# Seven products for eight in two column groups of each SwiGLU, in a float32 decoder trunk on one Trainium2 core

## The chip, the core and the metric

The kernel runs on one core of one Trainium2 chip. The core has a matrix engine (PE, with PEld for its weight loads), a vector engine (DVE), an activation engine (ACT), a general engine (POOL) and a sequencer (SP) that issues most transfers; sixteen DMA engines move the data. Each engine works through its own queue in order. The metric is the device time of one execution in microseconds (us), as a median of runs.

## What is computed

Two layers (DEPTH) over 256 tokens of width 1024. A layer is a half-step SwiGLU, a mixer of three branches, and a second half-step SwiGLU:

```python
def swiglu_ffn(h, w_in, w_out):
    gate, up = jnp.split(h @ w_in, 2, axis=-1)
    return (jax.nn.silu(gate) * up) @ w_out

for l in range(DEPTH):
    x = x + FFN_RESID * swiglu_ffn(rms_norm(x, ffn1_norm[l]), ffn1_w_in[l], ffn1_w_out[l])
...
    x = x + FFN_RESID * swiglu_ffn(rms_norm(x, ffn2_norm[l]), ffn2_w_in[l], ffn2_w_out[l])
```

w_in is 1024 x 5632 (2816 gate columns, then 2816 up columns), w_out 2816 x 1024, all in float32. So there are four SwiGLUs: a first and a second in each layer.

## The kernel before

**Precision.** Every large product is made of three matmuls in a rounded float32 (mm3x, L128): both operands are cut into a rounded high part and the rest, and high x high, high x low and low x high are added in PSUM. The weights are cut on the chip: split (L100) casts a chunk on ACT (whi, L106) and subtracts on DVE (wlo, L107).

**Stream.** All weights lie in one array, in the order of use, in chunks of at most 128 x 1024 (512 KB). load (L87) has SP fetch them into five raw buffers; prefetch cuts up to three chunks ahead of the one in use, into four whi and four wlo buffers. next_sub gives PE its next chunk.

**A SwiGLU** (ffn, L274). The first product runs over 11 groups of 512 columns, 256 of gate and the matching 256 of up. A group is four chunks; a chunk holds two row blocks of 128, and for each of them and each half of the tokens three matmuls of 512 columns are issued, twelve in all. Two PSUM banks (ps_in) collect the two token halves; acc has four banks, so that a group is read out while the next is computed. ACT makes SILU of the gate half (L302), DVE multiplies by up (L304); the result is turned by PE (ps_a, L269) and cut again (L270, L271) for the second product (ps_out), which adds to x.

**Norm.** rms_norm's gain goes into the cut of x (Norm.split: xg, L235 on ACT, L236 on DVE). The row factor rc = rs_x comes from sums of squares (xsq, L250) by POOL (L210) and is applied when a group is read out. The second half of x's columns is turned and cut only when the first chunk of the next stage has been issued (late).

**Order.** A scheduler lays out each engine's queue from the program's order and its own estimates; the splits have a higher priority. A tile's buffer is given by its tag, and a later tile with the same tag waits until the earlier one is done with: xbc, vg, zt, big12a and big12b are buffers that the mixer uses and a SwiGLU does not.

## Time and profile before

| | |
|---|---|
| median of 3 runs | 1265.35 us (1263.08 to 1266.62) |
| the profiled execution, its time | 1265.64 us |
| the profiled execution, its span | 1263.9 us |
| DVE, ACT busy | 63%, 53% of the span |
| weights and the rest read from HBM | 219.46 MB |

The page counts busy time by engine and cuts the span into 40 slices; DMA there is the mean busy share of the sixteen DMA engines:

```profile
DMA  8665564634554445555555555545455544555662
```

A row of a group reads: line, engine, operation, out<-in, shape, count, then busy us and mean ns of one, then the idle time of the engine just before, with what ended it. A row of the timeline reads: start, duration, engine, line, operation.

### The profile page before, as it was taken

To read this page: it belongs to the slowest core of one execution; us is meant where nothing else is said; L and a number is where in the kernel's file an instruction comes from. 1 tells how busy PE (TensorE), PEld (TensorE's weight loads), DVE (VectorE), ACT (ScalarE), POOL (GpSimd) and SP (SyncE) were. 2 spreads that over 40 slices of the span, in tenths; PEclk is the share of its full clock that TensorE was granted. 3 is DMA by queue.
4 is the path that set the end of the run, shared out by engine and by line. 5 is a ranking of instruction groups with operands and counts; after the bars stand their busy time and mean duration, and the time that the engine had idled before them with its cause. 6 is when DMAs were issued, how large, how long until landed. Compare 5 with 4: busy or idle time off the path is not lost.

```text
span 1263.9 us, 16712 instructions
## 1 busy us (share of the span) xinstructions
PE 1237.6 (98%) x6332; PEld 1042.4 (82%) x6332; DVE 791.8 (63%) x1099; ACT 667.9 (53%) x908; POOL 120.6 (10%) x108
## 2 busy tenths in 40 slices
PE   9999999999999999999999999999999999999998
PEld 6888889988887778888888888898988877888886
DVE  6555557888756665555556555588795576555553
ACT  7545445647666454444455444456567744545532
POOL 0000004423200000000000000064150000000000
PEclk9999999989999999999999999999999999999999
DMA  8665564634554445555555555545455544555662
GB/s 326 212 185 183 193 188 125 212 100 159 195 173 151 149 167 185 186 186 192 184 183 184 184 186 193 187 124 184 123 165 184 150 153 163 171 185 187 183 191 83
DMA packets 62432, 221.59 MB, mean 175 GB/s; under 512 B 7056, under 2 KB 7184, under 8 KB 62224
## 3 DMA queue, kind: packets, MB, share of 16 engines
q1 hardware_dynamic: 61488, 219.40, 52.9%
q10 hardware_dynamic: 864, 1.13, 0.3%
q8 instruction: 49, 0.80, 0.3%
q14 instruction: 31, 0.25, 0.1%
HBM read 219.46 MB, written 1.05 MB: 174 GB/s over the span
## 4 chain that ended last, share of the span: by engine, by line
PE 90%; DVE 4%; POOL 2%; issue 2%; ACT 1%; DMA 1%; SPq 0%; DVEq 0%; ACTq 0%; POOLq 0%
PE ps_in L131 12%; PE ps_in L130 12%; PE ps_in L132 12%; PE ps_out L132 7%; PE ps_out L130 7%; PE ps_out L131 7%; PE ps_g L131 3%; PE ps_g L130 3%; PE ps_g L132 3%; PE ps_in L126 2%; PE ps_in L124 2%; PE ps_in L125 2%; DVE wlo L107 2%; PE ps_a L269 2%; PE ps_br L130 1%
## 5 line engine op out<-in xcount | busy, mean ns | idle before, releaser
L107 DVE TENSOR_TENSOR wlo<-raw,whi 128x1024 fp32r<-128x1024 f32 (+3 forms) x417 | 513.6, 1235 | 364.8 <-ACT whi L106 363.7
L106 ACT CAST whi<-raw 128x1024 fp32r<-128x1024 f32 (+3 forms) x417 | 431.3, 1039 | 388.3 <-PE ps_in L132 156.4
L131 PE MATMUL ps_in<-wlo,xg 128*128 128x512 f32 x704 | 278.8, 396 | 0.9 <-DVE wlo L107 0.9
L130 PE MATMUL ps_in<-whi,xg 128*128 128x512 f32 x704 | 276.1, 396 | 2.2 <-ACT xg L235 1.2
L132 PE MATMUL ps_in<-whi,xg 128*128 128x512 f32 x704 | 273.6, 391 | 0.0
L130 PEld LDWEIGHTS ps_in<-whi,xg 128*128 128x128 f32 x704 | 131.9, 188 | 33.4 <-ACT whi L106 1.8
L131 PEld LDWEIGHTS ps_in<-wlo,xg 128*128 128x128 f32 x704 | 132.3, 188 | 27.2 <-DVE wlo L107 2.5
L132 PEld LDWEIGHTS ps_in<-whi,xg 128*128 128x128 f32 x704 | 132.0, 188 | 26.4
L126 PE MATMUL ps_in<-xg,wlo 128*128 128x256 f32 x336 | 96.4, 288 | 1.5 <-DVE wlo L107 1.5
L124 PE MATMUL ps_in<-xg,whi 128*128 128x256 f32 x336 | 95.1, 289 | 1.1 <-ACT whi L106 0.9
L125 PE MATMUL ps_in<-xg,whi 128*128 128x256 f32 x336 | 96.2, 288 | 0.0
L131 PE MATMUL ps_out<-wlo,aa 128*128 128x512 f32 x192 | 75.8, 395 | 0.0
L131 PE MATMUL ps_g<-wlo,xg 128*128 128x512 f32 x192 | 75.8, 395 | 0.0
L130 PE MATMUL ps_out<-whi,aa 128*128 128x512 f32 x192 | 75.5, 393 | 0.0
L132 PE MATMUL ps_g<-whi,xg 128*128 128x512 f32 x192 | 75.1, 391 | 0.0
L132 PE MATMUL ps_out<-whi,aa 128*128 128x512 f32 x192 | 74.8, 389 | 0.0
L210 POOL TENSOR_TENSOR rs_x<-ms_x,mhalf 128x2 f32<-128x2 f32 x6 | 4.2, 698 | 724.4 <-DVE ms_x L208 722.8
L130 PE MATMUL ps_g<-whi,xg 128*128 128x512 f32 x192 | 72.7, 394 | 0.0
L126 PEld LDWEIGHTS ps_in<-xg,wlo 128*128 128x128 f32 x336 | 65.3, 194 | 1.9 <-DVE wlo L107 1.9
L124 PEld LDWEIGHTS ps_in<-xg,whi 128*128 128x128 f32 x336 | 64.4, 194 | 2.0 <-ACT whi L106 1.9
L125 PEld LDWEIGHTS ps_in<-xg,whi 128*128 128x128 f32 x336 | 65.4, 195 | 0.7 <-issue 0.3
L130 PE MATMUL ps_out<-whi,ab 128*128 128x512 f32 x160 | 62.2, 389 | 0.0
(269 smaller groups left out, 1791.8 us busy)
## 6 DMA issues: line engine op xcount, KB each, us to landing
raw<-in_w SPq DMA_DIRECT2D x397, 512.0 KB, 3.5
raw<-in_w SPq DMA_DIRECT2D x8, 414.0 KB, 3.3
raw<-in_w SPq DMA_DIRECT2D x6, 384.0 KB, 3.0
raw<-in_w SPq DMA_DIRECT2D x4, 276.0 KB, 3.0
x<-in_xT SPq DMA_DIRECT2D x4, 256.0 KB, 4.7
x<-in_x SPq DMA_DIRECT2D x1, 1024.0 KB, 8.8
out_x<-x ACTq DMA_DIRECT2D x4, 256.0 KB, 3.7
row<-in_prow SPq DMA_DIRECT2D x2, 360.0 KB, 6.6
```

The lines of the kernel that those rows point to most:

```text
L106: act.copy(hi[:, a:b], r[:, a:b])
L107: dve.tensor_tensor(lo[:, a:b], r[:, a:b], hi[:, a:b].bitcast(F32), ALU.subtract)
L124: pe.matmul(ps, lhsT=whi, rhs=xhl[:, 0], start=first, stop=False)
L125: pe.matmul(ps, lhsT=whi, rhs=xhl[:, 1], start=False, stop=False)
L126: pe.matmul(ps, lhsT=wlo, rhs=xhl[:, 0], start=False, stop=last)
L130: pe.matmul(ps, lhsT=xhi, rhs=whi, start=first, stop=False)
L131: pe.matmul(ps, lhsT=xhi, rhs=wlo, start=False, stop=False)
L132: pe.matmul(ps, lhsT=xlo, rhs=whi, start=False, stop=last)
L210: pool.tensor_tensor(r, m, mhalf[:, :n], ALU.pow)
L269: pe.transpose(ps[:, i, halves(b)], parts[b][:, P * i : P * (i + 1)], ident)
```

## The change

The first product of each SwiGLU keeps seven of its eleven groups ("narrow", 28 chunks). The other four become two groups of 1024 columns ("wide", 512 of gate and 512 of up), computed by Strassen's form in Winograd's version. The tokens and the rows are halved, so that the input is x11, x12, x21, x22 (the first index is the token half; 128 tokens x 512 features each), and the weights of a wide group are b11, b12 (rows 0 to 511: gate, up) and b21, b22 (rows 512 to 1023). Instead of eight products of a block of x with a block of b there are seven, with b11, t1 = b11 + b12, t2 = b11 + b12 + b22, t3 = b12 + b22, b22, b21 and t4 = t2 + b21, the up columns carried with a minus sign that is taken back at the end (nrc). Each product is two chunks of six matmuls.

- **Weight sums.** t1 and t3 (tiles xsum, ysum) are made by transfers: SP loads b11 or b22 a second time, and POOL issues a transfer that adds b12 to it. t2 and t4 are made by DVE additions in place (L196, L189). All seven are cut like other chunks: a SwiGLU's first product has 56 splits, where it had 44. The raw buffers of b11 are held until t2 is made. SP fetches 40 raw chunks for it, where it had 44, and eight 512 KB loads for the sums; eight adding transfers follow on POOL.
- **Input sums.** Norm keeps a full copy of the scaled x (xgf, one more ACT activation for each block of 128 columns); combined forms four sums of its blocks on DVE and cuts them (xs).
- **Results.** Two banks of acc (ps_wa, ps_wd) are held by a wide group and accumulate several products; ACT copies ps_wa out in between (m, u, v), DVE adds ps_wd and ps_we. Two banks are left for a narrow group.
- **Order.** The wide products stand between narrow chunks: two narrow chunks behind each of the seven in the first wide group, and 2, 1, 1, 2, 1, 1, 2 in the second.
- aside and the turns of the results move to other places in the loop; the stream is packed in the new order.

The core of the diff:

```diff
+NARROW = 7
+WIDE = 2
+def _ffn_order():
+    narrow = [("n", g, c) for g in range(NARROW) for c in range(4)]
+    gaps = [[2] * 7, [2, 1, 1, 2, 1, 1, 2]]
+    order, narrow = narrow[:4], narrow[4:]
+    for j in range(WIDE):
+        for names, n in zip((("b11", "b12"), ("t1",), ("t2",), ("t3",), ("b22",), ("b21",), ("t4",)), gaps[j]):
+            order += [(name, j, c) for name in names for c in range(2)]
+            order += narrow[:n]
+            narrow = narrow[n:]
+    assert not narrow
+    return order
...
+    def load_sums(key, j):
+        tags = ("vg", "zt") if j == 0 else ("xbc", "xbc")
+        y = bp.tile([P, 2048], F32, name="ysum", tag="big12b") if j == 0 else sums[key, 0, "y"]
+        sums[key, j, "y"] = y
+        if j == 1:
+            both = bp.tile([P, 2, SUB_MAX], F32, name="xsum", tag="xbc")
+        for c in range(2):
+            x_ = bp.tile([P, SUB_MAX], F32, name="xsum", tag=tags[c]) if j == 0 else both[:, c]
+            sums[key, "t1", j, c] = x_
+            sums[key, "t3", j, c] = y[:, SUB_MAX * c : SUB_MAX * (c + 1)]
+        for name, base in (("t1", "b11"), ("t3", "b22")):
+            for c in range(2):
+                nc.sync.dma_start(out=sums[key, name, j, c], in_=source(chunk_at[key, (base, j, c)]))
+        for name in ("t1", "t3"):
+            for c in range(2):
+                pool.dma_start(out=sums[key, name, j, c], in_=source(chunk_at[key, ("b12", j, c)]), accum_op=ALU.add)
...
+    def split(u):
+        load(u + 1)
+        kind, key, i = units[u]
         with tc.high_priority():
+            if kind == "n":
+                splits[u] = parts_of(raws.pop(u), pieces(i))
+                return
+            key, (_, j, c) = key
+            full = ((0, SUB_MAX),)
+            if kind[0] == "b":
+                r = raws.pop(u)
+                splits[u] = parts_of(r, full)
+                if kind == "b11":
+                    held[c] = r
+                if kind == "b21":
+                    t = sums[key, "t1", j, c]
+                    dve.tensor_tensor(t, t, r, ALU.add)
+            elif kind == "t3":
+                splits[u] = parts_of(sums[key, "t3", j, c], full)
+            else:
+                t = sums[key, "t1", j, c]
+                splits[u] = parts_of(t, full)
+                if kind == "t1":
+                    dve.tensor_tensor(t, sums[key, "t3", j, c], held.pop(c), ALU.add)
...
         def split(self, j, src):
             g = self.gain[:, j : j + 1]
             act.activation(self.hl[:, j, 0], src, AF.Copy, scale=g)
+            if self.full is not None:
+                act.activation(self.full[:, j], src, AF.Copy, scale=g)
             dve.scalar_tensor_tensor(self.hl[:, j, 1], src, g, self.hl[:, j, 0].bitcast(F32), ALU.mult, ALU.subtract)
...
+    def combined(nrm, n, hi, lo):
+        x11, x21 = nrm.full[:, 0:4, 0:P], nrm.full[:, 0:4, P:]
+        x12, x22 = nrm.full[:, 4:8, 0:P], nrm.full[:, 4:8, P:]
+        if n == 0:
+            o = x22
+            dve.tensor_tensor(o, x22, x21, ALU.subtract)
+        elif n == 1:
+            o = x21
+            dve.tensor_tensor(o, x11, x21, ALU.subtract)
+        elif n == 2:
+            o = x11
+            dve.scalar_tensor_tensor(o, x22, -1.0, x11, ALU.mult, ALU.subtract)
+        else:
+            o = x12
+            dve.scalar_tensor_tensor(o, x11, -1.0, x12, ALU.mult, ALU.subtract)
+        act.copy(hi, o)
+        dve.tensor_tensor(lo, o, hi.bitcast(F32), ALU.subtract)
+        return hi, lo
...
+        def product(ps, xs, first):
+            for c in range(2):
                 hi, lo = next_sub()
                 for i in range(2):
                     k, w = 2 * c + i, slice(512 * i, 512 * (i + 1))
+                    xhi, xlo = xs(k)
+                    mm3x(ps, xhi, xlo, hi[:, w], lo[:, w], first and k == 0, k == 3, again=not first)
+        xs = {}
+        wide = {}
+        def snap(name, tag):
+            t = tp.tile([P, 512], F32, name=name, tag=tag, bufs=1 if tag == "ss" else 2)
+            act.copy(t, wide["A"])
+            return t
+        def gated(name, gate, b, up):
+            s = tp.tile([P, 512], F32, name="sw", tag="t")
+            act.activation(s, gate, AF.Silu, scale=nrm.rc[:, b : b + 1])
+            dve.scalar_tensor_tensor(up, up, nrm.nrc[:, b : b + 1], s, ALU.mult, ALU.mult)
+        def wide_step(kind, j):
+            if kind == "b11":
+                wide["A"] = acc.tile([P, 512], F32, name="ps_wa", tag="acc")
+                product(wide["A"], plain(0, 0), True)
+                wide["m"] = snap("m1", "ss")
+            elif kind == "t1":
+                wide["D"] = acc.tile([P, 512], F32, name="ps_wd", tag="acc")
+                product(wide["D"], summed(xs[0]), True)
+            elif kind == "t2":
+                product(wide["A"], summed(xs[2]), False)
+                wide["u"] = snap("u2", "xp")
+            elif kind == "t3":
+                product(wide["A"], summed(xs[1]), False)
+                wide["v"] = snap("u3", "xp")
+                dve.tensor_tensor(wide["v"], wide["v"], wide["D"], ALU.add)
+            elif kind == "b22":
+                product(wide["D"], summed(xs[3]), False)
+                dve.tensor_tensor(wide["u"], wide["u"], wide["D"], ALU.add)
+            elif kind == "b21":
+                e = mxp.tile([P, 512], F32, name="ps_we", tag="mx")
+                product(e, plain(1, 0), True)
+                dve.tensor_tensor(wide["m"], wide["m"], e, ALU.add)
+                gated("a0", wide["m"], 0, wide["u"])
+            else:
+                product(wide["A"], plain(1, 1), False)
+                gated("a1", wide["A"], 1, wide["v"])
+                for n in range(2):
+                    s = slice(256 * n, 256 * (n + 1))
+                    turns.append((2 * NARROW + 4 * j + 2 * n, [wide["u"][:, s], wide["v"][:, s]]))
...
+            if n == 0:
+                late()
+                nrm.finish()
+                load_sums(key, 0)
+                big = bp.tile([P, 3, 2, 4, P], F32R, name="xs", tag="big12a")
+                spots = [(big[:, m, 0], big[:, m, 1]) for m in range(3)]
+                spots.append([tp.tile([P, 4, P], F32R, name="xs", tag="prob") for _ in range(2)])
+            elif n in (1, 2):
+                for m in (0, 1) if n == 1 else (2, 3):
+                    xs[m] = combined(nrm, m, *spots[m])
+            turn_all()
...
+        for kind, g, c in _ffn_order():
+            if kind == "n":
+                gate, rows = np.arange(256 * g, 256 * (g + 1)), slice(256 * c, 256 * (c + 1))
+                cols = np.concatenate([gate, DFF + gate])
+            elif kind[0] == "b":
+                r = HD * (int(kind[1]) - 1) + 256 * c
+                o = 256 * NARROW + 512 * g + DFF * (int(kind[2]) - 1)
+                rows, cols = slice(r, r + 256), np.arange(o, o + 512)
+            else:
+                continue
+            wide(w_in[rows], cols)
```

Three places show how the queues change.

SP's queue at the start of the program, from the load of x on, before (x is the input, cs the constants, raw the weight chunks, row and ws parameters of the mixer):

```order
L154 DMA x<-in_x 128x2048
L159 DMA cs<-in_cst 128x912
L95 DMA raw<-in_w 128x1024 x2
L196 DMA row<-in_prow 128x720
L198 DMA ws<-in_ws 128x512
L95 DMA raw<-in_w 128x1024 x68
```

The same place after (xsum and ysum are the second loads of b11 and b22):

```order
L242 DMA x<-in_x 128x2048
L247 DMA cs<-in_cst 128x912
L160 DMA xsum<-in_w 128x1024 x2
L160 DMA ysum<-in_w 128x1024 x2
L141 DMA raw<-in_w 128x1024 x3
L284 DMA row<-in_prow 128x720
L286 DMA ws<-in_ws 128x512
L160 DMA xsum<-in_w 128x1024 x2
L141 DMA raw<-in_w 128x1024 x10
```

Six loads for sums now stand ahead of the eighth weight chunk, four of them ahead of the fifth.

DVE's queue in the middle of a first product, before (wlo is a split's second half, at the multiply of a group's results, aa their cut after the turn):

```order
L107 TENSOR_TENSOR wlo<-raw,whi 128x1024 x2
L271 TENSOR_TENSOR aa<-ps_a,aa 128x2x256
L107 TENSOR_TENSOR wlo<-raw,whi 128x1024
L304 SCALAR_TENSOR_TENSOR at<-ps_in,rs_x,s 128x256
L107 TENSOR_TENSOR wlo<-raw,whi 128x1024
L304 SCALAR_TENSOR_TENSOR at<-ps_in,rs_x,s 128x256
```

DVE's queue after, in the first SwiGLU, where t1 of the second wide group is cut and t2 is made (xsum<-ysum,raw):

```order
L170 TENSOR_TENSOR wlo<-xsum,whi 128x1024
L386 TENSOR_TENSOR ab<-ps_a,ab 128x2x256 x2
L196 TENSOR_TENSOR xsum<-ysum,raw 128x1024
L170 TENSOR_TENSOR wlo<-xsum,whi 128x1024
L170 TENSOR_TENSOR wlo<-raw,whi 128x1024
L196 TENSOR_TENSOR xsum<-ysum,raw 128x1024
L505 SCALAR_TENSOR_TENSOR at<-ps_in,rs_x,s 128x256
L170 TENSOR_TENSOR wlo<-xsum,whi 128x1024
L505 SCALAR_TENSOR_TENSOR at<-ps_in,rs_x,s 128x256
```

Between the turn and the two multiplies that free a narrow group's banks there are now two weight sums and more splits.

ACT's queue behind the first layer's mixer, where the norm's second half is cut, before (xsq are sums of squares):

```order
L250 ACTIVATE xsq,nss<-x 128x512
L235 ACTIVATE xg<-ps_x,pc 128x256 x4
L106 CAST whi<-raw 128x1024
L235 ACTIVATE xg<-ps_x,pc 128x256 x2
L106 CAST whi<-raw 128x1024 x3
```

The same place after:

```order
L342 ACTIVATE xsq,nss<-x 128x512
L325 ACTIVATE xg<-ps_x,pc 128x256
L327 ACTIVATE xgf<-ps_x,pc 128x256
L325 ACTIVATE xg<-ps_x,pc 128x256
L327 ACTIVATE xgf<-ps_x,pc 128x256
L325 ACTIVATE xg<-ps_x,pc 128x256
L327 ACTIVATE xgf<-ps_x,pc 128x256
```

Each xg is followed by its full copy before the next xg can start.

More of the change, by code (lines that the diff above doesn't have):

```diff
@@ L85, in pieces, with source @@
         return ((0, 512), (512, 1024)) if i == 0 else ((0, widths[i]),)
+    def source(i):
+        return wst[starts[i] : starts[i] + P * widths[i]].rearrange("(p n) -> p n", p=P)
     def load(n):
-        while st["load"] < min(n, len(widths)):
-            i = st["load"]
-            w = widths[i]
-            r = wp.tile([P, SUB_MAX], F32, name="raw", tag="raw", bufs=5)
-            src = wst[starts[i] : starts[i] + P * w].rearrange("(p n) -> p n", p=P)
-            for a, b in pieces(i):
-                nc.sync.dma_start(out=r[:, a:b], in_=src[:, a:b])
-            raws[i] = r
-            st["load"] += 1
@@ L99, in split @@
-    def split(i):
-        load(i + 1)
-        r = raws.pop(i)
+        while st["load"] < min(n, len(units)):
+            u = st["load"]
+            i = units[u][2]
+            if i is not None:
+                r = wp.tile([P, SUB_MAX], F32, name="raw", tag="raw", bufs=5)
+                for a, b in pieces(i):
+                    nc.sync.dma_start(out=r[:, a:b], in_=source(i)[:, a:b])
+                raws[u] = r
+            st["load"] += 1
+    sums, held = {}, {}
+    def load_sums(key, j):
[14 more added lines that the diff above has]
+                pool.dma_start(out=sums[key, name, j, c], in_=source(chunk_at[key, ("b12", j, c)]), accum_op=ALU.add)
@@ L110, in prefetch @@
     def prefetch(n):
         i = st["use"]
-        while st["split"] < min(i + n, len(widths)):
+        while st["split"] < min(i + n, len(units)):
             split(st["split"])
@@ L271, in turned, with ffn, turn, turn_all @@
         dve.tensor_tensor(lo, ps, hi.bitcast(F32), ALU.subtract)
[L274 to L278 removed]
+    def ffn(key, nrm, nxt, last, late, aside=None):
+        parts = [None, None]
         at = bp.tile([P, 2, 2, 256], F32, name="at", tag="ut")
[L280 to L285 removed]
+        turns = []
+        def turn(f, aa):
+            if parts[f // 12] is None:
+                parts[f // 12] = bp.tile([P, 12, 2, SEQ], F32R, name=f"a{'ab'[f // 12]}", tag=f"big24{'ab'[f // 12]}")
+            pt = mxp.tile([P, 2, SEQ], F32, name="ps_a", tag="mx")
+            o = parts[f // 12][:, f % 12 : f % 12 + 2]
+            turned(pt, aa, o[:, :, 0], o[:, :, 1])
+        def turn_all():
+            while turns:
+                turn(*turns.pop(0))
+        hl = nrm.hl
+        def plain(rows, toks):
+            return lambda k: (hl[:, 4 * rows + k, 0, halves(toks)], hl[:, 4 * rows + k, 1, halves(toks)])
+        def summed(t):
+            return lambda k: (t[0][:, k], t[1][:, k])
+        def product(ps, xs, first):
+            for c in range(2):
                 hi, lo = next_sub()
@@ L312, in ffn @@
+        ahl = [parts[f // 12][:, f % 12] if parts[f // 12] is not None else None for f in range(KF)]
         for h in range(2):
```

125 lines of the change are left out of this document (71 added, 54 removed).

## The prediction

> **What bounds the kernel now.** The page comes first: which engine is busy, and how evenly over the span.
>
> ```profile
> span 1263.9 us, 16712 instructions
> PE 1237.6 (98%) x6332; PEld 1042.4 (82%) x6332; DVE 791.8 (63%) x1099; ACT 667.9 (53%) x908; POOL 120.6 (10%) x108
> PE   9999999999999999999999999999999999999998
> ```
>
> TensorE (PE) is busy in every slice. A busy PE can still be a waiting one, so I read the timeline inside a first product next (start, duration, line, shape).
>
> ```profile
> 30.01 0.39 PE L130 MATMUL ps_in<-whi,xg 128*128 128x512 f32 x1
> ...
> 35.90 0.39 PE L131 MATMUL ps_in<-wlo,xg 128*128 128x512 f32 x1
> ```
>
> Between these two starts lie 26 steps, all alike: 5.89/26 = 0.2265 us. A 512-column matmul therefore costs 0.2265 us, not the 0.39 us of its own row, which overlaps the next. A chunk of twelve takes 2.72 us. Then the table by stages (busy time of PE, PEld, DVE, ACT, POOL; clock; DMA share; GB/s), for most of one first product and for the convolution stage behind it:
>
> ```profile
> 645.00:759.00 114.00, 114.00 (x523) 93.65 (x522) 64.90 (x73) 56.78 (x71) 0.00 (x0) 1.00 0.54 185
> 204.40:235.00 30.60, 28.39 (x225) 27.54 (x224) 27.02 (x29) 17.54 (x25) 23.99 (x26) 1.00 0.47 147
> ```
>
> In the first product PE never idles at the full granted clock (1.00), VectorE (DVE) has 57% and the DMA engines 54%. So fewer matmuls shorten this stage, as long as the new work fits into the free 43% of DVE. The second row shows the limit: at 88% DVE, PE lost 2.21 us of 30.60, 7.2%. Last, who waits for whom in the splits:
>
> ```profile
> L107 DVE TENSOR_TENSOR wlo<-raw,whi 128x1024 fp32r<-128x1024 f32 x397 | 490.3, 1238 | 357.3 <-ACT whi L106 356.1
> L106 ACT CAST whi<-raw 128x1024 fp32r<-128x1024 f32 x397 | 415.9, 1051 | 378.7 <-PE ps_in L132 156.4 <-PE ps_out L132 140.2 <-PE ps_g L132 27.1
> ```
>
> A split costs 1.05 us on ACT and 1.24 us on DVE, and the cast waits for PE to free a buffer: splits run ahead, PE sets the pace.
>
> **Term 1, the matmuls: -21.7 us.** Before, two groups of 1024 columns are 16 chunks, 192 matmuls. After, they are 2 x 7 products of 2 chunks with 6 matmuls, 168. Four first products save 4 x 24 = 96 matmuls of the same shape: 96 x 0.2265 = 21.7 us. The turns (PE transposes of at) stay 44 per product and cancel.
>
> **Term 2, the start: +11.2 us, between +6.0 and +16.3.** The first SwiGLU begins while the DMA engines are full:
>
> ```profile
> 15.00:18.00 3.00, 3.00 (x15) 2.49 (x14) 1.65 (x10) 3.00 (x9) 0.29 (x1) 1.00 1.03 410
> 21.00:24.00 3.00, 3.00 (x16) 2.46 (x15) 1.96 (x10) 2.96 (x5) 0.00 (x0) 1.00 1.04 411
> 16.05 0.29 POOL L174 CAST upr<-cs 128x128 fp32r<-128x128 f32 x1 [10.22 <-DMA cs<-in_cst]
> 17.37 1.05 ACT L106 CAST whi<-raw 128x1024 fp32r<-128x1024 f32 x1
> 25.39 0.61 PE L130 MATMUL ps_in<-whi,xg 128*128 128x512 f32 x2
> ```
>
> At 410 GB/s a 512 KB chunk takes 1.28 us of all engines. The constants landed at 16.05, the fifth chunk of weights 1.28 us later, and its cast starts at 17.37: the rate checks. At 25.39 the 73rd matmul of the program's stream starts (I count 24 from the fifth chunk on). In the changed SP queue, between the constants and the chunk that holds matmuls 73 to 84, stand xsum x2, ysum x2, raw x3, row (360 KB, 0.9 us), ws (256 KB, 0.64 us), xsum x2 and that chunk: ten loads, 12.8 + 1.5 = 14.3 us, so it lands at 30.4 us and its cast ends at 31.4. That is 6.0 us late even if adding transfers cost nothing. Four of them (xsum, ysum of the first group) are under way in the same time. No row shows an adding transfer or one issued by POOL; the nearest row is the plain load of the same 512 KB, 1.28 us, so four cost 5.1 us and the chunk's matmuls start at 36.6: 11.2 us late, which I take. If each reads for twice as long, 16.3. The extra ACT work of the first norm (8 more activations) and any late group 0 hide behind this wait: chunks five to seven, landed by 22.5 to 26, give PE only 5.4 us of work before it. What POOL pays for issuing is unknown; the bounds are 0 and its longest instruction in this trace, and rs_x stands behind two such issues:
>
> ```profile
> L210 POOL TENSOR_TENSOR rs_k<-ms_k,mhalf 128x16 f32<-128x16 f32 x2 | 9.4, 4684 | 4.8 <-DVE ms_k L208 4.8
> ```
>
> Two at 4.7 us would delay the first SILU to about 28 us and, through the turn that ACT has queued ahead of the next cast, the end of chunks five to seven to about 37, level with the wait: I take 0. In the other three products the sums of the first wide group are asked for before the product begins or at its start, and t1 stands six narrow and two wide chunks, 19 us, into it, at a DMA share of 0.54: 0.
>
> By the Trainium skill, "DMA: Bandwidth & Descriptors", section "Queues, rings and completion order", each DMA engine takes turns between the queues that have work; no row of before has two full queues, and if instead SP's loads went first, the 6.0 us above would be nearer.
>
> **Term 3, norms: +2 us (0 to 4).** At the start of a SwiGLU behind the mixer ACT is waited for:
>
> ```profile
> 448.41 1.56 ACT L235 ACTIVATE xg<-ps_x,pc 128x256 fp32r<-128x256 f32 x4
> 448.93 0.49 PE L130 MATMUL ps_in<-whi,xg 128*128 128x512 f32 x1 [0.58 <-ACT xg L235]
> ```
>
> The full-precision copy puts a second activation behind each, 1.56/4 = 0.39 us, so the second and third xg are 0.4 and 0.8 us later. Two such starts, and the SwiGLU behind a SwiGLU, where PE has no idle at all now: 0.8 + 0.8 + 0.4. The upper bound is all four extra activations on the path each time, 3 x 1.56 = 4.7, less PE work that can be done meanwhile.
>
> **Term 4, DVE and the accumulators in the wide stretches: +4 us (0 to 14).** Rows for the sum:
>
> ```profile
> L304 DVE SCALAR_TENSOR_TENSOR at<-ps_in,rs_x,s 128x256 f32<-128x256 f32 x88 | 42.2, 480 | 13.1 <-ACT s L302 13.1
> L302 ACT ACTIVATE s<-ps_in,rs_x 128x256 f32<-128x256 f32 x88 | 41.3, 470 | 38.0 <-PE ps_in L132 37.7 <-POOL rs_x L210 0.2
> L271 DVE TENSOR_TENSOR aa<-ps_a,aa 128x512 fp32r<-128x512 f32 x24 | 16.6, 691 | 6.9 <-ACT aa L270 6.9
> 26.28 4.62 DVE L107 TENSOR_TENSOR wlo<-raw,whi 128x1024 fp32r<-128x1024 f32 x4
> ```
>
> The second wide group is the tight one. PE: 14 chunks of 6 and 10 of 12 matmuls, 46.2 us, with the turns about 47.7. DVE: 24 splits (29.7), 4 weight sums at the split's price (5.0), 4 evictions (1.9), 4 turns (2.8), 3 additions from PSUM and 2 gates at 0.69 (3.5): 42.9 us, 90%. The first wide group has 28 splits and four more narrow chunks: about 49 of 58.7 us, 83%. Split by split this fits: a cast for the chunk four ahead can start as soon as PE ends a chunk, 1.05 + 1.24 us later the chunk is ready, and PE still holds three chunks, at least 5.4 us. Back to back DVE is even quicker (4.62/4 = 1.16). ACT has 24 x 1.05 + 3 copies and 2 SILUs at 0.59 + 4 x 0.47 + 4 x 0.59 = 32 us, 68%: no bound. The place without slack is the accumulator: two of four banks are held by the wide group, so a narrow group must be read out before the next starts, within one wide product, 12 x 0.2265 = 2.72 us. SILU and multiply of the first half, a split between, and the second half take about 3.2 us (2 x 0.47 + 2 x 0.48 + 1.24), and the second half is needed 0.7 us after the first: 0 by this sum, but any weight sum (1.24 us) queued ahead shows. I take 0.5 us at each of two boundaries, 1 us per product, 4 in all. The upper end is the 7.2% of the convolution stage on 4 x 47.7 us: 13.7.
>
> **Sum.** -21.7 + 11.2 + 2 + 4 = -4.5 us on the profiled execution's 1265.64 us (its span of 1263.9 and 1.7 around it; the median of the runs is 1265.35, the same within 0.02%): **1261 us**. By itself this case reaches from 1257 to 1265.
>
> **Rivals.**
> - *Adding transfers cost double* (an engine reads the old sum as well as the new chunk). Eight loads' time for four: 16.3 instead of 11.2, hence 1266 us, no change that can be measured. For it: the sum must be read back from SBUF. Against it: no row shows whether reads or writes fill the engines. "Collectives: The Full Stack" of the Trainium skill, section "The bandwidth ceiling: the fold count and why AG ≠ RS ≠ AR", says that an add in the DMA path halves the rate because of its two source reads; no run here shows it yet, and by it the sum would be this 1266.
> - *DVE becomes the bound* in the second wide group. Mechanism: one in-order queue holds splits, weight sums, gates and evictions; one late eviction keeps a PSUM bank, PE stops, and the split it was to free comes late too. Price: 7.2% of 47.7 us, four times, 13.7 instead of 4: 1271 us, slower. It decides once a stretch loses 3 us or more (12 in all). For it: 90% is above the 88% that cost PE 2.21 us. Against it: in that stage DVE's work was shared with POOL's 23.99 us and had a chain of its own; the SwiGLU has neither. If the double transfers join it: 1276.
> - *The start costs only the loads*, with adding transfers beside them, and the stretches flow: -21.7 + 6.0 + 1 + 0 = -14.7, 1251 us. Against it: the engines are at 1.03 already, so nothing has room beside them.
>
> **How the numbers follow.** Forecast 0.40, double transfers 0.15, DVE 0.25, cheap start 0.20. A measurement of this kernel can tell about 0.3%, 3.8 us: below 1261.6 is faster, above 1269.1 slower. The forecast's case lies astride the first bound, 0.25 and 0.15. Faster: 0.20 + 0.25 = 0.45; same: 0.15 + 0.15 = 0.30; slower: 0.25. The range runs from the cheap start's floor (-21.7 + 6.0, 1250) to DVE with double transfers, 1276.
>
> **What would show it.** Term 1: 96 fewer 512-column matmuls at the same 0.2265 us pitch. Term 2: around 25 to 37 us PE idle before the eighth chunk, released by the cast that waits for a DMA; the 73rd matmul at 36.6. An adding transfer's share of the DMA queue, per byte, against a load's decides between 1x and 2x. Term 3: xg waits of PE of 1 to 1.4 us behind the mixer. Term 4: DVE near 90% in the second half of each first product, PE idle there below 1 us, or above 3 us if the rival holds, released by DVE. The prediction is wrong if an adding transfer takes so long that later products wait for their sums as well, or if the mixer's POOL work, behind two such issues, turns late.

## The result, and the profile after

The changed kernel takes 1301.16 us (median of 4 runs, 1293.88 to 1308.02) beside 1264.21 us of the kernel before on the same chip: a ratio of 1.0289, 95% interval 1.0216 to 1.0361. It is slower, by 37 us, where 1261 us were forecast. Its profiled execution took 1295.77 us, nearer to its fastest run than to the median; all sums below are made against that execution's span, 1293.7 us, 29.8 us above the 1263.9 us of before. The four runs scatter by 14 us, and the two longer ones have the lower mean clock (0.978 and 0.975 beside 0.987 and 0.984); where a median is compared with this kernel's, the difference of the profiled spans is given beside it.

The page of the changed kernel, the rows that answer to those of before:

```profile
span 1293.7 us, 16828 instructions
...
PE 1234.4 (95%) x6236; PEld 1032.4 (80%) x6236; DVE 904.4 (70%) x1223; ACT 740.9 (57%) x1011; POOL 145.2 (11%) x140
...
PEclk8899999999999999899999999999999999999999
...
q1 hardware_dynamic: 63792, 227.79, 52.0%
q0 software_dynamic: 4608, 16.78, 7.1%
...
PE 80%; DVE 7%; DMA 5%; ACT 3%; issue 3%; POOL 1%; ACTq 0%; DVEq 0%
```

There are 96 matmuls fewer, as planned, but PE's busy time fell by only 3.2 us instead of 21.7, and its idle time rose from 26.3 (1263.9 - 1237.6) to 59.3 us. So the 29.8 us are +33.0 of idle time and -3.2 of busy time; 18.5 us of the saving went into matmuls that run slower. The row PEclk shows most of why: the granted clock (the part of TensorE's full speed that was allowed) is below 9 tenths in three slices, and its mean over the span is 0.984 (0.996 before). Taken over PE's busy time in steps of 0.5 us, the clock costs 17.4 us of work, 5.1 before, so some 12 of the 18.5 us. The rest is not clock: in the third SwiGLU, where it stays at 1.00, PE's busy time falls by 4.1 us (187.1 to 183.0) instead of 5.4, and where that goes was not traced. The last row is the chain that ended last: DMA has 5% of it, 1% before.

Where the time lies, by PE's timeline (length of each SwiGLU from its first matmul, the first from the start of the program, to the first matmul of the next stage or the end):

| SwiGLU | 1 | 2 | 3 | 4 |
|---|---|---|---|---|
| before | 194.8 | 188.3 | 187.1 | 192.2 |
| changed | 214.7 | 195.8 | 185.2 | 197.6 |
| difference | +19.9 | +7.5 | -1.9 | +5.4 |
| lost, beside the 5.4 us of matmuls that each saves | 25.3 | 12.9 | 3.5 | 10.8 |

The two mixers together are 1.1 us shorter. So half of the 52 us lost lie in the first SwiGLU, and most of the rest in the second and fourth. First the start of the first one: the changed kernel's table by stages (columns as before: busy time of PE, PEld, DVE, ACT, POOL; clock; DMA share; GB/s).

```profile
24.00:27.00 3.00, 0.98 (x2) 0.47 (x3) 1.92 (x2) 2.32 (x3) 0.00 (x0) 0.55 1.06 280
27.00:30.00 3.00, 3.00 (x8) 2.32 (x9) 1.23 (x1) 0.24 (x2) 0.00 (x0) 0.50 1.03 260
...
33.00:36.00 3.00, 1.04 (x3) 0.85 (x4) 2.18 (x10) 0.68 (x2) 0.00 (x0) 0.76 1.05 257
...
39.00:42.00 3.00, 0.00 (x0) 0.00 (x0) 0.00 (x0) 1.03 (x2) 1.75 (x2) 0.89 1.05 410
42.00:45.00 3.00, 2.89 (x6) 1.90 (x7) 2.95 (x3) 2.86 (x4) 0.00 (x0) 0.50 1.07 220
```

And PE's timeline at the eighth chunk:

```profile
42.07 1.22 PE L218 MATMUL ps_in<-whi,xg 128*128 128x512 f32 x2 [3.17 <-ACT whi L169]
```

The engines are full (share above 1.0) from 24 to 45 us, but while adding transfers run they move 220 to 280 GB/s instead of 410; the 220 are from 42 to 45 us, where POOL's queue has nearly all of the engines' time. The eighth chunk's matmuls start at 42.07 us; 25.39 us was the 73rd matmul before, 36.6 the forecast. And the clock is 0.50 behind each stall: 27 to 30 us has 8 matmuls in 3 us, where 3 us held 14 or 15 before.

Then the later products: who waits for whom (total, times, longest, in us), and the place of PE's longest wait for `at`, in the second SwiGLU, on PE and on DVE.

```profile
ACT whi L169 <- DMA raw<-in_w: 28.9, 13, 6.8
...
DVE xsum L189 <- DMA raw<-in_w: 25.1, 9, 6.6
...
PE ps_in L218 <- DVE at L505: 14.6, 5, 5.2
...
PE ps_x L336 <- DVE xg L328: 4.3, 2, 2.2
```

```profile
516.58 0.40 PE L220 MATMUL ps_wd<-whi,xs 128*128 128x512 f32 x1
522.22 0.80 PE L218 MATMUL ps_in<-whi,xg 128*128 128x512 f32 x1 [5.24 <-DVE at L505]
522.81 0.63 PE L219 MATMUL ps_in<-wlo,xg 128*128 128x512 f32 x1
523.24 0.63 PE L220 MATMUL ps_in<-whi,xg 128*128 128x512 f32 x1
```

```profile
511.00 0.68 DVE L453 TENSOR_TENSOR u<-u,ps_wd 128x512 f32<-128x512 f32 x1
518.27 1.22 DVE L189 TENSOR_TENSOR xsum<-xsum,raw 128x1024 f32<-128x1024 f32 x1 [6.59 <-DMA raw<-in_w]
...
521.68 0.48 DVE L505 SCALAR_TENSOR_TENSOR at<-ps_in,rs_x,s 128x256 f32<-128x256 f32 x1
...
523.21 0.48 DVE L505 SCALAR_TENSOR_TENSOR at<-ps_in,rs_x,s 128x256 f32<-128x256 f32 x1
```

Read the three fences together. PE waits 5.24 us for `at`, the multiply that reads a finished narrow group out of its banks. `at` needs only PSUM and a SILU, but DVE's queue has the weight sum t4 (L189) ahead of it, and that sum waits 6.59 us for the raw chunk b21. Behind the stall the matmuls start 0.43 us apart (522.81, 523.24) instead of 0.2265.

### The profile page after: what moved, and what is told of

It reads as the page before. It is cut to its first block, busy times and chain, and to the rows that moved or that the text cites. A ratio compares the mean times of both kernels' runs of the same rounds, so it can differ in the third digit from the quotient of the medians.

```text
span 1293.7 us, 16828 instructions
## 1 busy us (share of the span) xinstructions
PE 1234.4 (95%) x6236; PEld 1032.4 (80%) x6236; DVE 904.4 (70%) x1223; ACT 740.9 (57%) x1011; POOL 145.2 (11%) x140
## 3 DMA queue, kind: packets, MB, share of 16 engines
q0 software_dynamic: 4608, 16.78, 7.1%
## 4 chain that ended last, share of the span: by engine, by line
PE 80%; DVE 7%; DMA 5%; ACT 3%; issue 3%; POOL 1%; ACTq 0%; DVEq 0%
PE ps_out L220 7%; PE ps_out L218 7%; PE ps_out L219 7%; PE ps_in L218 7%; PE ps_in L220 7%; PE ps_in L219 7%; DMA raw<-in_w 5%; PE ps_g L219 3%; PE ps_g L218 3%; PE ps_g L220 3%; DVE wlo L170 3%; PE ps_wa L220 2%; PE ps_wa L218 2%; PE ps_wa L219 2%; PE ps_in L212 2%
## 5 line engine op out<-in xcount | busy, mean ns | idle before, releaser
L170 DVE TENSOR_TENSOR wlo<-raw,whi 128x1024 fp32r<-128x1024 f32 (+3 forms) x401 | 491.9, 1231 | 250.7 <-ACT whi L169 246.3
L169 ACT CAST whi<-raw 128x1024 fp32r<-128x1024 f32 (+3 forms) x401 | 414.3, 1038 | 355.0 <-PE ps_out L220 139.0
L218 PE MATMUL ps_in<-whi,xg 128*128 128x512 f32 x448 | 172.0, 408 | 20.0 <-DVE at L505 14.6
L219 PE MATMUL ps_in<-wlo,xg 128*128 128x512 f32 x448 | 178.6, 399 | 5.6 <-DVE wlo L170 5.6
L220 PE MATMUL ps_in<-whi,xg 128*128 128x512 f32 x448 | 176.7, 399 | 2.7 <-DVE xg L328 2.7
L218 PEld LDWEIGHTS ps_in<-whi,xg 128*128 128x128 f32 x448 | 84.6, 192 | 40.9 <-DVE at L505 16.8
L219 PEld LDWEIGHTS ps_in<-wlo,xg 128*128 128x128 f32 x448 | 86.2, 192 | 25.6 <-DVE wlo L170 8.5
L220 PEld LDWEIGHTS ps_in<-whi,xg 128*128 128x128 f32 x448 | 85.7, 192 | 21.2 <-DVE xg L328 3.2
L220 PE MATMUL ps_out<-whi,aa 128*128 128x512 f32 x192 | 76.6, 399 | 0.0
L218 PE MATMUL ps_out<-whi,aa 128*128 128x512 f32 x192 | 76.4, 398 | 0.0
L220 PE MATMUL ps_out<-whi,ab 128*128 128x512 f32 x160 | 62.3, 389 | 0.0
L218 PE MATMUL ps_out<-whi,ab 128*128 128x512 f32 x160 | 62.3, 389 | 0.0
```

The source lines that it names most:

```text
L169: act.copy(hi[:, a:b], r[:, a:b])
L170: dve.tensor_tensor(lo[:, a:b], r[:, a:b], hi[:, a:b].bitcast(F32), ALU.subtract)
L218: pe.matmul(ps, lhsT=xhi, rhs=whi, start=first, stop=False, skip_group_check=again)
L219: pe.matmul(ps, lhsT=xhi, rhs=wlo, start=False, stop=False, skip_group_check=again)
L220: pe.matmul(ps, lhsT=xlo, rhs=whi, start=False, stop=last, skip_group_check=again)
```

## The experiments

Each was timed against the kernel before on its own chip. Theory A in what follows: the adding transfers' time in the DMA engines makes the loss, at the start and later. Rival B: DVE's load does.

**1. The first SwiGLU narrow again, the other three wide** (e1).

```diff
-NARROW = 7
-WIDE = 2
+def _wide(key):
+    return 0 if key == (0, 0) else 2
+def _narrow(key):
+    return KF // 2 - 2 * _wide(key)
```

> The first SwiGLU of the program is put back to eleven narrow groups, the other three keep two wide groups. Theory A (the start): of the 29.8 us that the changed kernel's span is longer, 20.1 lie between the program's start and the mixer's first product, because the sums' transfers stand ahead of the eighth chunk while the DMA engines are full. Then this kernel runs in 1295.8 - 20.1, about 1276 us, and the 73rd matmul starts near 25.4 us again. Rival B (each wide product loses alike by DVE and the accumulators, 52.6 us of loss over four products): 13 us less loss and 5.4 us more matmuls, about 1288 us.

Measured: 1282.7 us, ratio 1.0142 (1.0116 to 1.0167); the first SwiGLU takes 195.4 us, the others 196.0, 187.9 and 197.3. 18.5 us come back (16.1 between the profiled spans), less than theory A's 20 and more than B's 8. The stages decide: the first SwiGLU alone is 19.3 us shorter, and the other three lose about as much as in the changed kernel, where B had each of the four lose alike. So the start is half of it, not all.

**2. No adding transfers** (e2), **or plain ones in their place** (e3).

```diff
-                pool.dma_start(out=sums[key, name, j, c], in_=..., accum_op=ALU.add)
 # e3:
+                pool.dma_start(out=sums[key, name, j, c], in_=...)
```

> The sixteen adding transfers are left out, so t1 and t3 are b11 and b22 alone (the outputs change by that; all matmuls, loads, weight sums and gates stay). Theory A (an adding transfer holds the DMA engines for two loads, 2.56 us): the eighth chunk comes some 10 us earlier, near 32 us, and later chunks no longer wait in the second wide group's sums; together 15 to 25 us less, 1271 to 1281 us. Rival B (DVE's queue bounds the wide stretches): only the start gains, about 10 us, 1286 us. Rival C (an adding transfer costs a plain one): about 5 us less at the start, 1290 us.

> The sixteen transfers stay where they are, issued by POOL, but overwrite instead of adding (t1 and t3 become b12 alone; the outputs change by that). Theory A (adding doubles the engines' time): this takes half of what leaving them out saves, 1283 to 1289 us, and a transfer of POOL's queue takes the same share of the DMA engines per byte as one of SP's. Rival C (adding is as cheap as overwriting, the price lies in the bytes and in POOL's issue): no change from the changed kernel, 1296 us, at a share per byte still near 1.85 times a load's.

Measured: 1260.6 us without them (ratio 0.9974, 0.9956 to 0.9991), 1276.09 us with plain ones (1.0093, 1.0067 to 1.0119). From the changed kernel's 1301.16, the adding costs 25 us and the bytes 15.5 (22.3 and 14.6 between the profiled spans): both runs came out below theory A's ranges, on the side away from its rivals. Without them, PE's row of the page, then one of the waits:

```profile
PE 1219.8 (97%) x6236; PEld 1022.9 (81%) x6236; DVE 904.8 (72%) x1223; ACT 740.5 (59%) x1011; POOL 119.8 (10%) x108
```

```profile
PE ps_in L215 <- DVE at L502: 1.7, 3, 1.0
```

With plain ones, the page's row of POOL's queue, then PE's timeline at the eighth chunk:

```profile
q0 software_dynamic: 4608, 16.78, 3.8%
```

```profile
37.38 0.87 PE L218 MATMUL ps_in<-whi,xg 128*128 128x512 f32 x2 [3.06 <-ACT whi L169]
```

Three readings. DVE has the same 904.8 us of work and PE waits 1.7 instead of 14.6 us for `at`: DVE's load alone does not bound, so rival B falls for these stretches. A plain transfer from POOL takes 3.8% x 1271.4 / 16.78 = 2.9 us of 16 engines per MB, an adding one 7.1% x 1293.7 / 16.78 = 5.5: 1.9 times. And with plain transfers the eighth chunk starts at 37.38 us, where the prediction had put it (36.6) at the price of one load; the engines move 405 to 411 GB/s from 24 to 39 us there.

**3. The transfers alone: the kernel before with six loads and six adding transfers that nobody reads** (e4).

```diff
                         nrm.finish()
+                        extra()
+        for n, t in enumerate(to):      # xsum x2, ysum x2, xsum x2
+            nc.sync.dma_start(out=t, in_=source(8 + n))
+        for n, t in enumerate(to):
+            pool.dma_start(out=t, in_=source(16 + n), accum_op=ALU.add)
```

> The kernel before, with all narrow groups, and six loads and six adding transfers that nobody reads, issued at the place in the first SwiGLU where the changed kernel issues its first six. Theory A (the transfers alone make the start's loss): the 73rd matmul starts near 42 us as in the changed kernel, PE's granted clock falls behind the stall, and the time is 1264 + 17 to 25, 1281 to 1289 us. Rival D (the start's loss is the added work of ACT and DVE in the first norm and the combined inputs): at most the 8 to 10 us that twelve plain loads cost, 1274 us or less.

Measured: 1283.87 us, ratio 1.0151 (1.0128 to 1.0174), 19 us. PE's row of its page, then PE's timeline at the eighth chunk:

```profile
PE 1246.9 (97%) x6332; PEld 1047.6 (82%) x6332; DVE 792.9 (62%) x1099; ACT 666.8 (52%) x907; POOL 124.5 (10%) x114
```

```profile
42.90 0.73 PE L133 MATMUL ps_in<-whi,xg 128*128 128x512 f32 x2 [2.47 <-ACT whi L109]
```

The eighth chunk comes at 42.90 us (42.07 in the changed kernel), with no Strassen work at all. Against before, PE's idle time is 10.5 us longer (1283.7 - 1246.9 against 26.3) and its busy time 9.3 us, for the same matmuls: the stalls cost their length and nearly as much again in slower matmuls.

**4. Stalls without transfers: chunks held back by POOL in the kernel before** (e12).

```diff
         r = raws.pop(i)
+        for _ in range(HOLD.get(i, 0)):    # 4, 5, 6, 8 copies in the four SwiGLUs
+            pool.tensor_copy(r, r)
```

> The kernel before, with one chunk in the middle of each first product held back by POOL (4, 5, 6 and 8 copies of the chunk onto itself), so that PE stalls four times for different lengths, with no other transfer. Theory H (a stall of PE costs its length and a stretch at half the granted clock behind it): behind a stall of 2.8 us or more the 512-column matmuls start about 0.43 us apart for 1.3 to 6 us, and each stall costs 1 to 3 us more than its length; behind one below 1.5 us the pitch stays 0.2265 us. Rival (the low clock belongs to the DMA load or to the start of the program): the clock stays at 1.00 behind these stalls.

Measured: 1278.53 us, ratio 1.0114 (1.0092 to 1.0136). The first hold was hidden, the others stalled PE. Table by stages, second and third SwiGLU, then PE's timeline behind the third's longest idle time:

```profile
515.00:517.50 2.50, 1.76 (x8) 0.99 (x6) 0.97 (x2) 1.51 (x3) 0.00 (x0) 1.00 0.00 0
517.50:520.00 2.50, 1.96 (x9) 1.29 (x10) 2.09 (x2) 2.50 (x4) 0.00 (x0) 1.00 0.00 0
...
705.00:707.50 2.50, 1.48 (x7) 0.63 (x5) 0.97 (x2) 1.14 (x3) 0.00 (x0) 1.00 0.00 0
707.50:710.00 2.50, 1.14 (x2) 0.50 (x2) 1.85 (x3) 2.50 (x4) 0.00 (x0) 0.77 0.00 0
710.00:712.50 2.50, 2.46 (x7) 1.96 (x7) 2.50 (x4) 1.64 (x2) 0.00 (x0) 0.54 0.58 185
```

```profile
708.86 1.22 PE L134 MATMUL ps_in<-whi,xg 128*128 128x512 f32 x2 [1.62 <-ACT whi L110]
```

Idle for 0.74 + 0.54 us within 5 us, the clock stays at 1.00; idle for 1.02 + 1.36 us, it falls to 0.5 until about 712 us, and the DMA engines are at rest when it falls. So the rival is out and theory H holds in its core, but not with its lengths: the longest single stall here is 1.62 us (the timeline's row), not 2.8. Over the whole execution PE has 5.8 us more idle and 5.7 us more busy time than before.

No limit on idle time can be read from these traces. With the extra transfers (e4), 0.94 + 0.76 us of idle around 882 us were followed by a clock of 0.50; the same two waits of the kernel before, 0.94 + 0.76 us around 861 us, left it at 1.00. One wait of 2.23 us in the mixer (for its tile aseg, to 259.79 us) cost the kernel before 7.5 us at 0.50; in the run without adding transfers the same wait of 2.23 us cost nothing, and a gap of 2.93 us in e11 (to 1142.91 us) cost nothing either. What the runs do show is the price of a fall that no new stall prolongs: 3.5 to 4 us, or 7 to 7.5 us, at half the clock, which is 1.7 or 3.4 us of PE's work when PE is busy throughout. The Trainium skill, "TensorE: Matmul & The Clock Gate", section "Part 1: The HAM clock gate", says that the array runs at half its clock after an idle window of about 3.4 us and until about as long a busy one has passed; the half clock and the shorter stretch of 3.5 to 4 us agree, the length of the idle time does not: 1.70 us within 3 us were enough in e4.

**5. The weight sums, the norm copies and the burst, one at a time** (e7, e6, e11).

```diff
 # e7: t2 and t4
-                    dve.tensor_tensor(t, t, r, ALU.add)
+                    pool.tensor_tensor(t, t, r, ALU.add)
 # e6
-                act.activation(self.full[:, j], src, AF.Copy, scale=g)
+                pool.tensor_tensor(self.full[:, j], hi, lo, ALU.add)
 # e11, behind the products b11, t2, t3, b22 of the first wide group, one pair each
+        pool.tensor_copy(t[:, 0:1], gate[:, 0:1])
         nc.sync.dma_start(out=t, in_=...)
         pool.dma_start(out=t, in_=..., accum_op=ALU.add)
```

> The weight sums t2 and t4 (32 additions of 128x1024, 1.22 us each on DVE) are moved to POOL; the adding transfers stay. Theory A (transfers bound the wide stretches; DVE's sum only stands where a late raw chunk is waited for): little is won, 0 to 8 us, and the waits for raw chunks stay. Rival B (DVE's load of 90% bounds the wide stretches): DVE loses 39 us of work, and most of the 13 us of loss in the later three products and of that behind the start goes: 15 us or more, below 1286 us.

> The full-precision copy xgf of the norm is no longer written by a second ACT activation but by POOL as hi + lo. Theory A (the copies on ACT delay the transposes at a SwiGLU's start, the idle of PE rises from 0.58 to 3.5 us behind a mixer): some 2.5 us less at each of two starts and up to 1 us behind a SwiGLU, 1295 us against the changed kernel's 1301. Rival (DVE's xg subtraction and not ACT holds the bank ps_x): no change, and PE still waits for xg of DVE for 2 us at each of these starts.

> The changed kernel, but the four pairs of load and adding transfer for the second wide group are asked for one at a time, behind the products b11, t2, t3 and b22 of the first group (POOL copies one column as a gate). All transfers and all work of DVE, ACT and PE stay. Theory A1 (raw chunks that are issued beside two adding transfers in a row take 9 to 10 us instead of 3.5, and the stall follows from this burst): the waits of DVE and PE in the middle of the products go, 12 to 20 us less, 1281 to 1289 us. Theory A2 (the total of the engines' time counts, not the burst): no more than 5 us less, above 1296 us.

Measured: 1281.45 (ratio 1.0125, 1.0104 to 1.0147), 1278.05 (1.0098, 1.008 to 1.0117) and 1285.4 us (1.0179, 1.0147 to 1.021). The first is B's number, but not by B's cause, since DVE's busy time did not fall (915.1 us beside 904.4; the last section says why). The second, 23 us less (17.1 by the spans), is three to four times the 6 us that the norms lose (below), outside both of its expectations. In each of these two, 4 us of the gain lie in the first SwiGLU (210.5 us). The third is in A1's range, but not for A1's reason alone: PE's wait for `at` stayed (12.8 us), and 3.6 of its 12.3 us of span come from the start, which lost two xsum loads. In e7 and e6 that wait shrank, to 3.1 and 3.3 us. What e6 had changed besides the copies is seen on DVE in the second SwiGLU: the sum t4 stood behind one more split, its chunk was there, and `at` followed at once. So the two cures had one thing in common, no late sum ahead of `at`; that is theory D.

**6. The sum t4 behind the multiply, and nothing else** (e13).

```diff
-                    dve.tensor_tensor(t, t, r, ALU.add)
+                    with tc.issue_after(marks[-1].ins):   # the last at multiply
+                        dve.tensor_tensor(t, t, r, ALU.add)
```

> The changed kernel with one edit: the sum t4 on DVE stands behind the two multiplies at<-ps_in,rs_x,s of the narrow group that ended last, instead of ahead of them; nothing else of the work or the transfers is changed. Theory D (the stall inside the products needs both: a raw chunk delayed by adding transfers, and a sum that waits for it ahead of the multiply that frees PE's banks): PE's wait for the multiply (14.6 us) goes nearly altogether with the slow clock behind it, 15 to 22 us less, 1279 to 1286 us. Rival R (the late chunk stalls PE in any case, since its own product waits): PE's wait only moves to ps_we<-whi, less than 6 us won, above 1295 us.

Measured: 1272.89 us, ratio 1.0082 (1.0054 to 1.011): 28 us less than the changed kernel (22.7 by the spans of the profiled executions) for a sum that moved behind four rows of DVE's queue; theory D had 15 to 22, 1279 to 1286 us. Of the 22.7 us, 3.1 lie in the second mixer, which the edit does not touch. PE's wait for `at`, 14.6 us in the changed kernel, and the same place on DVE:

```profile
PE ps_in L219 <- DVE at L506: 1.0, 1, 1.0
```

```profile
506.27 0.68 DVE L454 TENSOR_TENSOR u<-u,ps_wd 128x512 f32<-128x512 f32 x1
...
509.31 0.48 DVE L506 SCALAR_TENSOR_TENSOR at<-ps_in,rs_x,s 128x256 f32<-128x256 f32 x1 [0.23 <-ACT s L504]
...
511.71 0.48 DVE L506 SCALAR_TENSOR_TENSOR at<-ps_in,rs_x,s 128x256 f32<-128x256 f32 x1
513.14 1.23 DVE L190 TENSOR_TENSOR xsum<-xsum,raw 128x1024 f32<-128x1024 f32 x1 [0.95 <-DMA raw<-in_w]
516.73 1.23 DVE L190 TENSOR_TENSOR xsum<-xsum,raw 128x1024 f32<-128x1024 f32 x1 [2.37 <-DMA raw<-in_w]
```

The sum still waits for its raw chunk (0.95 and 2.37 us), but the multiplies that free PE's banks no longer stand behind it. Rival R falls: the chunk is late, and its own product can bear it (from 500 to 520 us PE idles 0.69 us, where ps_we waits). The four SwiGLUs take 208.8, 190.0, 183.8 and 191.0 us; what remains is mostly the start, though it too is 5.9 us shorter than in the changed kernel.

Why the chunk is late is seen in the changed kernel's DMA view for 507 to 513 us (share of the 16 engines, then the median from issue to landing):

```profile
q0 software_dynamic: 148, 0.56, 51.6%
q1 hardware_dynamic: 154, 0.56, 40.8%
issues: line engine op xcount, KB each, median us to landing
raw<-in_w SPq DMA_DIRECT2D x3, 512.0 KB, 9.6
ysum<-in_w POOLq DMA_DIRECT2D x2, 512.0 KB, 8.7
```

Beside two adding transfers a raw chunk takes 9.6 us; the page's median is 3.9. The two queues share the engines nearly evenly; the rule of the Trainium skill that the prediction cited ("DMA: Bandwidth & Descriptors", section "Queues, rings and completion order"), that engines take turns between queues with work, agrees.

**7. Sums by POOL instead of adding transfers** (e5, e8, e9, e10). b12 is loaded once, POOL adds it to b11 and b22.

```diff
 # e9, e10: b12 straight into xsum (e5, e8: into a buffer of its own)
-        for name, base in (("t1", "b11"), ("t3", "b22")):
+        for name, base in (("t1", "b12"), ("t3", "b22")):
-                pool.dma_start(..., accum_op=ALU.add)
+            pool.tensor_tensor(sums[key, "t3", j, c], sums[key, "t3", j, c], sums[key, "t1", j, c], ALU.add)
+                    pool.tensor_tensor(t, t, r, ALU.add)    # t = xsum, r = b11
```

> No adding transfer: the chunk b12 is loaded once by a plain transfer into a buffer of its own, and POOL adds it to b11 (xsum) and to b22 (ysum), 8 additions of 128x1024 a product; loads of a wide group fall from 14 chunks, 4 of them adding at the price of two, to 10. Theory A (the changed kernel loses by the DMA engines' time): the time is that of the run without adding transfers or a little below, since two loads fewer stand at the start: 1252 to 1263 us. Rival B (POOL's additions, 2.4 us each by yhl<-zt,yhl, come late or slow DVE beside them): the sums are waited for, 1270 us or more.

> First SwiGLU all narrow, sums of the other three by POOL from plain loads, xgf by POOL. Theory A (start, adding transfers and norm copies are the three losses, and they add up): the time before, less 3 x 5.4 us of matmuls, plus up to 2 us a product of remaining waits: 1249 to 1256 us, below both kernels. Rival (the losses only move, from the DMA engines to POOL and DVE): 1262 us or more, no faster than before.

> As the run with the first SwiGLU narrow and POOL's sums, but with no buffer and no late load for b12: it is loaded by a plain transfer straight into xsum, POOL adds it to ysum (b22) and then adds b11 to it in place; xgf by POOL. Theory A (the loss of that run, 17.5 us of PE's waits for casts of xsum in ps_wd, came from b12 being loaded behind the chunk buffers and not from POOL's additions): the waits at t1 go, each wide product is 3 to 5 us shorter than a narrow one, 1249 to 1257 us, below both kernels. Rival (POOL's additions slow DVE and ACT whenever they run): 1265 us or more.

> The same sums in place, with two wide groups in all four SwiGLUs. Theory A: the start still has four loads ahead of the eighth chunk, so its first SwiGLU is like that of the run without adding transfers, 200 us instead of 194.8, and the whole is 4 to 7 us above the kernel with the narrow first SwiGLU: 1254 to 1263 us. Rival: above 1270 us, if POOL's additions stand in each other's way at the start.

Measured: 1322.87 and 1313.22 us with the extra buffer, 1284.95 and 1293.7 us in place. All four expectations failed, on the rivals' side. With the extra buffer PE waits 17.5 us for the casts of xsum (e8, `PE ps_wd L239 <- ACT whi L186: 17.5, 6, 5.6`; 11.5 us in e5). In place most of that goes, but DVE slows beside POOL. DVE's splits of raw chunks and POOL's additions in the run with the narrow first SwiGLU (e9):

```profile
L176 DVE TENSOR_TENSOR wlo<-raw,whi 128x1024 fp32r<-128x1024 f32 x385 | 501.6, 1309 | 244.0 <-ACT whi L175 242.0
L194 POOL TENSOR_TENSOR xsum<-xsum,raw 128x1024 f32<-128x1024 f32 x12 | 36.7, 3069 | 60.0 <-DMA raw<-in_w 59.8
```

A split takes 1309 ns in the mean (1236 in the changed kernel), an addition 3.07 us. DVE's busy time is 920.1 us against 876.3 of the first experiment, whose matmuls and first SwiGLU are the same. Here rival B's mechanism, a DVE near its limit, may have come true; it was not separated from the order of its queue.

**8. What is left when the causes are taken away** (e14 to e17): the first SwiGLU narrow and xgf by POOL (e15), the sum t4 behind as well (e14), the pairs one at a time as well (e16), and one wide group late in the first SwiGLU (e17).

```diff
 # e14: e1 + e6 + e13;  e15: e1 + e6;  e16: e14 + e11
 # e17: e14 with _wide((0, 0)) = 1, 16 narrow chunks ahead of it, and
+                if _wide(key) == 1 and g == 1:
+                    load_sums(key, 0, aa[1])       # gated on at
```

> First SwiGLU narrow, xgf by POOL, and the sum t4 behind the multiplies; adding transfers as in the changed kernel. If the three losses (start, norm copies, DVE's order) are those of the changed kernel, each of the three wide products lies between the 184 to 190 us of the run without adding transfers and 3 us more: 1253 to 1262 us, at or a little below the kernel before. Rival (other waits take their place): 1268 us or more.

> The same without the edit on the sum t4: first SwiGLU narrow and xgf by POOL alone. By the stages of the run with xgf by POOL (190.5, 183.4 and 190.2 us for its last three SwiGLUs) and the narrow first of 195 us: 1258 to 1266 us. It tells whether the edit on the sum is worth anything beside the moved norm copies; if theory D holds and the moved copies had also put the sum behind, the two kernels are within 3 us.

> The kernel of the three edits, with the second wide group's pairs of load and adding transfer asked for one at a time as well. If what is left of the loss is the raw chunks beside pairs of adding transfers, 2 to 6 us below the kernel of the three edits, 1250 to 1258 us; if SP's queue held by the gates costs as much as the burst did, the same or 1 to 4 us more.

> The kernel of the three edits, but the first SwiGLU has one wide group instead of none, behind four narrow ones, and its sums are asked for only behind the second narrow group (a gate of POOL on at), when the start's transfers are long through. If the start's loss was only the place of the transfers, the first SwiGLU is 0.5 to 2.7 us shorter than the 195.3 us of the narrow one and the time 1256 to 1260 us. If adding transfers cost more than a wide group saves wherever they stand, it is 196 us or more and the time 1260 us or more.

| kernel | us, median | ratio to before, 95% |
|---|---|---|
| e14 | 1259.49 | 0.9974 (0.9961 to 0.9988) |
| e15 | 1261.84 | 0.9981 (0.9967 to 0.9995) |
| e16 | 1260.6 | 0.9977 (0.9965 to 0.9989) |
| e17 | 1259.78 | 0.9970 (0.9958 to 0.9983) |

All four are a little below the kernel before, by 0.2 to 0.3%, and not told apart from each other. The edit on t4 adds little once xgf is on POOL, as e15's expectation had it. Asking one at a time adds nothing then. In the last one the first SwiGLU takes 199.5 us beside 195.3 for the narrow one: its PE idles 5.9 us between 10 and 30 us, waiting for DVE and ACT, which have the first norm's extra work; whether that work could be placed better was not tried. That is the length that e17's rival named (196 us or more), but not by its cause: the sums' transfers are issued only from 41 us on. Of the 5.4 us of matmuls that each product saves, e14 keeps 4.2 us over three. Most of the missing 12 us is no idle time: at nearly the clock of before (0.995 beside 0.996), PE's busy time falls by 6.3 us (1237.6 to 1231.3) instead of 16.3. Why was not traced.

## Why the prediction was wrong, step by step

- **Term 1 (matmuls, -21.7 us): right in its count and pitch**, 96 fewer at the same 0.2265 us where PE does not stall. What it left out, without a reason given, is that the pitch is no constant: 18.5 us of the saving went into slower matmuls, some 12 of them in half-clock stretches.
- **Term 2 (the start, +11.2) was mis-sized, by its price of an adding transfer.** The first SwiGLU lost 25.3 us where the terms had 12.2. The sum took one load's time, 36.6 us for the eighth chunk; with plain transfers that chunk came at 37.38, with adding ones at 42.07. The rival "adding transfers cost double" had 36.6 + 5.1 = 41.7 and was the right one here; "Collectives: The Full Stack" of the Trainium skill, section "The bandwidth ceiling: the fold count and why AG ≠ RS ≠ AR", says this of a reduction between cores, and the transfers here agree (1.9 times by the queue's share). But that rival too ended at 1266, because it as well left out the clock and the other three products: the twelve transfers alone cost 10.5 us of idle and 9.3 us of slower matmuls.
- **"In the other three products ... 0" is the step that failed.** It looked at t1, which has 19 us of time, and at a DMA share of 0.54. It did not ask what the transfers do to the raw chunks beside them: 9.6 us instead of 3.9 to land. These three products lost 27 us; the terms for norms and DVE had 5 of them.
- **Term 3 (norms, +2, 0 to 4) was too small.** In the 12 us behind each mixer PE idles 3.5 and 3.8 us (0.58 before, where the waits name one xg), about 6 us more; the second activation holds ps_x, and with it two transposes and the next matmuls. At the start of the third SwiGLU PE has no idle time. With xgf on POOL (e6) the waits for ps_x are gone and the idle time is 0.55 and 0.76 us.
- **Term 4 (DVE and the accumulators, +4, 0 to 14) named the place and missed the price.** It said that "any weight sum (1.24 us) queued ahead shows". What showed was not the sum's 1.24 us but its wait for a transfer, up to 6.59 us, with the slow clock behind it; e13 won 28 us (22.7 by the spans) by moving it. DVE's 90%, on which the second rival rested, cost little by itself (1.7 us of waits at the same load without adding transfers).
- **The listed signs were near.** PE idle above 3 us, released by DVE, came, but as the sign of a rival whose reason, DVE's load, was not the one; the queue's share per byte decided the price; and "an adding transfer takes so long that later products wait for their sums as well" named the transfers but not the wait, which was for raw chunks beside them. Each stood alone; the sum needed them together: transfer, queue order and clock.

## What to carry to other kernels

Price a stall of PE at its length and, from about 2 us of idle time on, at a possible 1.7 to 3.4 us more for the slow matmuls behind it; in these runs the idle time alone did not tell which stall paid. When transfers are added beside a stream of loads, look at the stream: with the engines full, each load behind the new transfers lands later, and the first in-order queue that waits for one passes the delay on to everything behind it. So an instruction that waits for a transfer must not stand ahead of one that frees a PSUM bank, and that order is worth reading on its own, since unrelated edits change it.

## What the runs showed of the hardware

- An adding transfer from HBM into SBUF takes 5.5 us of 16 engines per MB, a plain one from the same queue 2.9, and the rate falls from 410 GB/s to between 220 and 280 while adding ones run.
- The granted clock falls to half behind idle gaps of 1.02 and 1.36 us within 5 us, with no transfer under way, and stays there for 3.5 to 4 us; 0.74 and 0.54 us left it at 1.00. Between 1.7 us of idle time (e4, a fall) and 2.93 us (e11, none), the runs show both.
- DVE's splits of 128x1024 take longer beside additions of that size on POOL. With the 32 weight sums on POOL (e7) the mean of a split rises from 1236 to 1330 ns:

```profile
L170 DVE TENSOR_TENSOR wlo<-raw,whi 128x1024 fp32r<-128x1024 f32 x381 | 505.0, 1330 | 240.2 <-ACT whi L169 236.4
L189 POOL TENSOR_TENSOR xsum<-xsum,raw 128x1024 f32<-128x1024 f32 x16 | 44.6, 2791 | 71.9 <-DMA raw<-in_w 65.2 <-DVE at L505 6.6
```

  Of the 39 us that DVE gave away, its splits of raw chunks took back some 36 (381 x 0.094) and those of xsum some 6 (48 x 0.128), and DVE's busy time rose from 904.4 to 915.1 us. An addition on POOL takes 2.8 us in this row; the only other one of this shape, yhl<-zt,yhl in the mixer of the changed kernel, takes 2.4.
